# Three placements of sums, copies and weight splits around the seven-product projections of a one-core decoder layer

## The chip, the core and the metric

The kernel runs on one core of a Trainium2 chip. Its engines are called PE (matrix products), DVE and ACT (element-wise work), POOL, and SP (which issues the loads); each works through its own list of instructions in order. The metric is device time in microseconds (us) of one execution. Lower is better.

## What is computed

One layer: a norm, a combined input projection, three branches (attention, convolution, short convolution), a sum of the branches under sigmoid gates, an output projection with a residual, a second norm and a gated feed-forward part with a residual. The part that matters here:

```python
merged = g[:, :, 0] * y_a + g[:, :, 1] * y_b + g[:, :, 2] * y_c
x = x + merged @ w_o[l]
hf = rms_norm(x, ffn_norm_g[l]) @ w_ffn_in[l]
gt, up = jnp.split(hf, 2, axis=-1)
x = x + (jax.nn.silu(gt) * up) @ w_ffn_out[l]
```

There are 512 positions and 1024 channels; `w_o` is 1024 x 1024, `w_ffn_out` 2816 x 1024, all in f32.

## The kernel before

**Products.** A f32 operand is kept as two rounded tiles, a high part and a low part. ACT makes the high one with a cast (L81), DVE the low one with a subtraction (L82), and `mm3` (L92 on) makes one f32 product of three matmuls: high x high, low x high, high x low. In the records the weight's parts are `wh` and `wl`, and a matmul of 128x512 of any of these products is a row of L90.

**Seven products.** `merged @ w_o` and both halves of the last projection are cut into 2 x 2 blocks and done as a Strassen-like scheme of seven products instead of eight. The contraction goes in pairs of 128 rows: four pairs for `w_o`, six and then five for `w_ffn_out`. In what follows (j, p) is product p of pair j: two banks of three matmuls, six rows of L90. Block sums of the left side are made by `quarters` (L554 on), of the weights by DVE from the pieces b11, b12, b21, b22 of a pair. Products 1, 6 and 7 come first. At the change (`middle`, L606 on) ACT and DVE read their banks: the bank of product 7 gets -7 - (1 + 6), two new banks p5 are filled with the sum 1 + 6, and copies of product 7's old content (s7) are kept and added to the residual by `rest`. Products 2, 4, 5 and 3 then accumulate on top of what the banks hold, so product 4 of any pair needs the change of p7 done.

**Order.** PE's order is the one in which the code calls (`manual_schedule`). DVE, ACT, POOL and SP are ordered by a scheduler by priority; `tc.issue_after(i)` keeps an instruction behind i, `tc.high_priority` puts it forward. Each tile belongs to a ring of a few buffers (`wh` and `wl` three each, `raw` three), so a split also waits until PE has read the split that held its buffer.

**Around the change.** The last branch is `branch(1, ..., last=True)`: sixteen units, a gate and a product for each of eight column blocks. Behind its thirteenth unit stands `first_sums(0)`, which loads b11, b12 and b22 of pair 0 of `w_o` and forms t3 = b22 - b12 and t2 = t3 + b11 (L791, L792). For pairs 1 to 3 `first_sums` is called after the branch. PE's order there is (0,1), then (1,1), (0,6), (0,7), then (2,1), (1,6), (1,7), then (3,1), (2,6), (2,7), (3,6), (3,7), the change, and (0,2), (0,4), (1,2), (1,4) and so on (L853 on); t2 - b21 (L856) is the weight of product 4. Products 5 and 3 follow with the weight sums of L871, between them four transposes (`turn`, L819; its records are L822) for the second norm, and four more transposes after the first twelve matmuls of the feed-forward part. The residual adds are L862, L864, L884, L885 and L887; L624 is the add of `rest`. In `ffn_out` the sums for products 5 and 4 are L954 to L956, and the last two pairs of its second call are taken product by product, (3,5), (4,5), (3,3), (4,3), (3,4), (4,4), (3,2), (4,2); the final adds and stores are L986 and L988.

Of the kernel before, what the change touches and what calls it, by code (L numbers as in the profile page):

```python
# [35 lines left out]
def hybrid_layer(ctx, tc, x, mix_norm_g, w_in, q_norm_g, k_norm_g, w_attn_out, conf_dw_w,  # L36
# [537 lines left out]

    def seventh(a, w, banks, start):
        for i in range(2):
            mm3(banks[i], [t[:, i * P:(i + 1) * P] for t in a], w, start, True)
# [28 lines left out]
    def middle(p1, p6, p7):  # L606
# [4 lines left out]
        with tc.high_priority(offset=PRIO):  # L611
            for i in range(2):
                s1 = tmp()
                nc.scalar.copy(s1, p1[i])
                nc.vector.tensor_add(s2[i], p6[i], s1)
                nc.scalar.copy(p5[i], s2[i])
            for i in range(2):
                s7.append(tmp())
                nc.scalar.copy(s7[i], p7[i])
                change = nc.vector.scalar_tensor_tensor(p7[i], p7[i], -1.0, s2[i], ALU.mult,  # L620
                                                        ALU.subtract)
        def rest():
            for i in range(2):
                nc.vector.tensor_add(x1_at(i + 2, 1), s7[i], x1_at(i + 2, 1))  # L624
# [6 lines left out]
    def branch(g, w, a, last=False):  # L631
        for f4 in range(0, KT, 4):
            wy = once(lambda f4=f4: raw(w[:, f4 * P:(f4 + 4) * P], CT, 4 * P))
            for f2 in range(f4, f4 + 4, 2):
                wg = in_raw(4096 + g * D + f2 * P)
                for j in range(2):
# [7 lines left out]
                    def product(y, f=f, s=s):  # L644
                        if f not in merged:
# [126 lines left out]
    def after(*ins):  # L772
        stack = ExitStack()
        stack.enter_context(tc.high_priority())
        for i in ins:
            stack.enter_context(tc.issue_after(i))
        return stack

    def first_sums(j):
# [9 lines left out]
        with after(*last_sum):  # L789
            t3, t2 = tmp(), alloc("c")  # L790
# [16 lines left out]
    queue += units[:13] + [call(lambda: first_sums(0))] + units[13:]  # L807
# [32 lines left out]
    for j in range(n):  # L840
        if j:
            first_sums(j)
# [10 lines left out]
    b21 = [wo_piece(j, 1, 0) for j in range(n)]  # L853
    for j in range(n):
        with after(*[change][:j]):
            nc.vector.tensor_sub(t2s[j], t2s[j], b21[j])  # L856
# [10 lines left out]
    for j in range(n):  # L867
        b11, b12, b22 = wo_raw[j]
        with after(*[half][:j]):
            t1 = alloc("c")  # L870
            nc.vector.tensor_sub(t1, b12, b11)  # L871
        held.append(parts2(b22, t1))
        if j == 1:
            rest()
# [8 lines left out]
    for i in range(2):  # L883
        nc.vector.tensor_add(x1_at(i + 2, 1), x1_at(i + 2, 1), p5[i])  # L884
        nc.vector.tensor_add(x1_at(i, 1), x1_at(i, 1), p5[i])  # L885
    for i in range(2):
        nc.vector.tensor_add(x1_at(i, 1), x1_at(i, 1), p3[i])  # L887
# [41 lines left out]
    def ffn_out(j0, h, last):  # L929
# [23 lines left out]
        def t14(t1, t4):  # L953
            nc.vector.tensor_sub(t1, b12, b11)  # L954
            nc.vector.tensor_sub(t4, b22, b21)  # L955
            nc.vector.tensor_sub(t4, t4, t1)  # L956
# [3 lines left out]
        ends = n - 2 if last else n  # L960
        pieces, ws = [], []
        for j in range(n + 1):
            if j < n:
# [4 lines left out]
                pieces.append(w)  # L968
                two, three = parts(w[:, 1], "u" if last and j == n - 1 else None)
                ws.append({2: two, 3: three})  # L970
            if j:
                (b11, b12), (b21, b22) = [[pieces[j - 1][:, k, i] for i in range(2)]
                                          for k in range(2)]
                t1, t4 = parts(sums(t14, *[change][:j - 1]), "u" if last and j == n else None)
                ws[j - 1].update({5: t1, 4: t4})
            if j == 2:
                rest()
            now = [(j, p) for p in (2, 3) if j < ends] + [(j - 1, p) for p in (5, 4)
                                                          if 0 < j <= ends]
            if last and j == n:  # L980
                now = [(i, p) for p in (5, 3, 4, 2) for i in (n - 2, n - 1)]
            for i, p in now:
# [71 lines left out]
```

## Time and profile before

| | |
|---|---|
| median of three runs | 840.54 us (840.12 to 843.98) |
| the profiled execution | 839.71 us, its span 838.0 us |
| granted PE clock, mean | 0.997 |
| DVE / ACT busy | 76% / 49% of the span |
| stage of `w_o`, PE records | from 435.64 us to 482.95 us of the span |
| second call of `ffn_out`, from product 5 of pair 2 on | from 817.6 us to the end |

The records of PE overlap: a matmul of 128x512 is recorded with 0.39 us and the next one starts 0.23 us after it, so a busy share near 98% hides short waits, which are read from start times in the timeline and from the list of waits.

### The profile page before, as it was taken

The page shows a single profiled execution, that of the slowest core. Times are in us where ns is not written, and L with a number is a line of the kernel's source. Part 1 is how long each engine was busy: PE and PEld are TensorE (multiplying, and loading weights), DVE is VectorE, ACT ScalarE, POOL GpSimd, SP SyncE. Part 2 cuts the span into 40 slices and gives each one's busy share as a digit, 9 for nine tenths or more (in the row PEclk, how much of TensorE's full clock was granted, in tenths as well). Part 3 has the DMA queues.
Part 4 walks back from the last instruction along what each step waited for, and adds up shares of the span by engine and source line. Part 5 has one row for each costly group of instructions (what it writes and reads, how often), then busy time and mean ns, then how long its engine had stood idle before and what let it go on. Part 6 is the DMA issues. An engine that isn't in the chain of part 4 may idle for free.

```text
span 838.0 us, 9783 instructions
## 1 busy us (share of the span) xinstructions
PE 818.6 (98%) x3703; PEld 677.9 (81%) x3703; DVE 635.0 (76%) x952; ACT 410.9 (49%) x621; POOL 36.2 (4%) x60
## 2 busy tenths in 40 slices
PE   6999999999999999999998999999999999999997
PEld 6887887888888888888886778888888888888885
DVE  6598799897899999776578857555679865556796
ACT  6345698877664232573345554333345423333461
POOL 3100010002100000000000040000000000000000
PEclk9999999999999999999999999999999999999999
DMA  7333114112113143143241433332235733322452
GB/s 252 104 101 99 53 50 151 51 51 101 51 51 101 51 151 101 51 142 110 88 163 50 151 101 100 101 101 88 75 113 201 251 101 101 101 88 76 139 187 101
DMA packets 71468, 90.13 MB, mean 108 GB/s; under 512 B 2112, under 2 KB 56572, under 8 KB 71420
## 3 DMA queue, kind: packets, MB, share of 16 engines
q1 hardware_dynamic: 70252, 87.40, 31.3%
q10 hardware_dynamic: 1168, 2.10, 0.6%
q8 instruction: 29, 0.48, 0.2%
q14 instruction: 19, 0.16, 0.1%
HBM read 87.39 MB, written 2.10 MB: 107 GB/s over the span
## 4 chain that ended last, share of the span: by engine, by line
PE 89%; DVE 7%; issue 2%; ACT 1%; DMA 1%; SPq 0%; DVEq 0%; ACTq 0%
PE mm L90 75%; PE z L90 10%; PE o L90 3%; DVE wl L82 2%; DMA u<-in_w_o_dram 1%; ACT wh L81 1%; PE mm L297 1%; DVE cf L503 0%; DMA m<-in_x_dram 0%; PE z L297 0%; PE mm L822 0%; DVE tt L955 0%; DVE tt L956 0%; DVE tt L954 0%; DVE t L791 0%
## 5 line engine op out<-in xcount | busy, mean ns | idle before, releaser
L90 PE MATMUL mm<-u,wh 128*128 128x512 f32 x1536 | 474.9, 390 | 0.0
L90 PEld LDWEIGHTS mm<-u,wh 128*128 128x128 f32 x1536 | 287.2, 188 | 59.5 <-DVE u L304 0.6
L90 PE MATMUL mm<-u,wl 128*128 128x512 f32 x768 | 299.2, 390 | 0.0
L81 ACT CAST wh<-raw 128x1024 fp32r<-128x1024 f32 (+1 forms) x150 | 140.5, 937 | 240.5 <-PE mm L90 194.4
L82 DVE TENSOR_TENSOR wl<-raw,wh 128x1024 fp32r<-128x1024 f32 (+1 forms) x148 | 161.0, 1088 | 37.6 <-ACT wh L81 36.9
L90 PEld LDWEIGHTS mm<-u,wl 128*128 128x128 f32 x768 | 144.1, 188 | 30.1
L503 DVE SCALAR_TENSOR_TENSOR cf<-cf,cols_w,cf 128x512 f32<-128x512 f32 x120 | 89.8, 749 | 3.7 <-ACT cf L501 1.2
L916 DVE TENSOR_TENSOR t<-mm,cf 128x512 f32<-128x512 f32 x22 | 15.2, 691 | 59.7 <-PE mm L90 59.7
L90 PE MATMUL mm<-m,wh 128*128 128x512 f32 x128 | 39.4, 389 | 0.0
L81 ACT CAST wh<-tt 128x1024 fp32r<-128x1024 f32 x21 | 22.1, 1053 | 31.0 <-PE mm L90 16.5
L914 DVE TENSOR_TENSOR t<-mm,cf 128x512 f32<-128x512 f32 x22 | 15.1, 687 | 25.5 <-PE mm L90 25.4
L90 PE MATMUL mm<-wh,m 128*128 128x512 f32 x88 | 29.6, 392 | 0.0
L90 PEld LDWEIGHTS mm<-m,wh 128*128 128x128 f32 x128 | 24.0, 188 | 4.9
L82 DVE TENSOR_TENSOR wl<-tt,wh 128x1024 fp32r<-128x1024 f32 x21 | 25.6, 1220 | 2.9 <-ACT wh L81 2.8
L78 ACT ACTIVATE s<-s 128x384 f32<-128x384 f32 (+1 forms) x48 | 26.9, 561 | 1.1
L90 PE MATMUL z<-wh,m 128*128 128x512 f32 x72 | 26.0, 393 | 0.8 <-DVE z L620 0.8
L90 PE MATMUL mm<-m,wl 128*128 128x512 f32 x64 | 24.9, 389 | 0.0
L449 DVE SCALAR_TENSOR_TENSOR s<-z,s 128x384 f32<-128x384 f32 (+1 forms) x24 | 14.3, 598 | 11.6 <-ACT s L78 10.4
L834 POOL TENSOR_TENSOR cf<-cf,t 128x512 f32<-128x512 f32 x7 | 11.0, 1576 | 257.3 <-ACT t L832 257.1
L81 ACT CAST m<-t 128x512 fp32r<-128x512 f32 x21 | 13.1, 623 | 17.7 <-DVE t L560 11.3
L78 ACT ACTIVATE t<-t 128x512 f32<-128x512 f32 x31 | 19.6, 631 | 3.7 <-DVE t L914 3.6
L90 PEld LDWEIGHTS mm<-wh,m 128*128 128x128 f32 x88 | 16.8, 191 | 3.6
(301 smaller groups left out, 1135.6 us busy)
## 6 DMA issues: line engine op xcount, KB each, us to landing
raw<-in_w_in_dram SPq DMA_DIRECT2D x23, 1024.0 KB
raw<-in_w_ffn_in_dram SPq DMA_DIRECT2D x22, 1024.0 KB
raw<-in_w_ffn_out_dram SPq DMA_DIRECT2D x11, 1024.0 KB
raw<-in_w_ffn_out_dram SPq DMA_DIRECT2D x11, 512.0 KB
raw<-in_w_in_dram SPq DMA_DIRECT2D x10, 512.0 KB
raw<-in_w_ffn_out_dram SPq DMA_DIRECT2D x11, 256.0 KB
raw<-in_w_o_dram SPq DMA_DIRECT2D x9, 256.0 KB
m<-in_x_dram SPq DMA_DIRECT2D x8, 256.0 KB
```

Source lines behind the costliest of these rows:

```text
L78: table(nc.scalar.activation(o, i, f, **kw))
L81: (copy or nc.scalar.copy)(hi, src)
L82: return (sub or nc.vector.tensor_sub)(lo, src, hi.bitcast(F32))
L90: nc.tensor.matmul(o, lhsT, rhs, start=start, stop=stop, skip_group_check=True)
L297: nc.tensor.matmul(pts[f][:, t * P:(t + 1) * P], xblock(xt, t, f), diag, start=True, stop=True, skip_group_check=True)
L449: marks.append(nc.vector.scalar_tensor_tensor(t, z, 0.0, t, ALU.max, ALU.add))
L503: nc.vector.scalar_tensor_tensor(y, pad[:, n:n + S], w(n), y, ALU.mult, ALU.add)
L834: nc.gpsimd.tensor_add(sumsq, sumsq, s)
L914: nc.vector.tensor_mul(g, pg[0], rstd[0])
L916: nc.vector.tensor_mul(u, pu, rstd[0])
```

## The change

It reorders work and changes no product. It has five parts.

1. `first_sums(0)`, `(1)`, `(2)` are called between the last three units of the last branch instead of one before them and the others behind; t3 lies in the ring `cf` instead of `t`; the multiply of the very last product of the branch is kept behind the newest of these sums.
2. In `middle` the two copies into p5 come after the change of p7, and `rest` is kept behind a given instruction.
3. In `w_o`, product 4 of pair j is called behind product 2 of pair j + 1, all four t2 - b21 are kept behind the change (before: all but the first), and the sums t1 = b12 - b11 of pairs 0 to 2 are formed ahead of the first residual adds.
4. The last residual adds of `w_o` get a high priority.
5. In `ffn_out` the sums for products 5 and 4 are chained in the pairs' order, and for the last two pairs of the second call the weights of products 5 and 4 are split ahead of those of 2 and 3. PE's order in `ffn_out` stays.

```diff
@@ middle
                 nc.vector.tensor_add(s2[i], p6[i], s1)
-                nc.scalar.copy(p5[i], s2[i])
+            behind = []
             for i in range(2):
                 s7.append(tmp())
-                nc.scalar.copy(s7[i], p7[i])
-                change = nc.vector.scalar_tensor_tensor(p7[i], p7[i], -1.0, s2[i], ALU.mult,
-                                                        ALU.subtract)
-        def rest():
+                copied = nc.scalar.copy(s7[i], p7[i])
+                with after(*behind):
+                    change = nc.vector.scalar_tensor_tensor(p7[i], p7[i], -1.0, s2[i], ALU.mult,
+                                                            ALU.subtract)
+                behind = [change.ins]
+            with after(copied.ins):
+                for i in range(2):
+                    nc.scalar.copy(p5[i], s2[i])
+        def rest(*behind):
...
@@ branch
                     def product(y, f=f, s=s):
-                        if f not in merged:
+                        if last and f == KT - 1:
+                            with after(*last_sum):
+                                nc.vector.tensor_mul(s[0], y, s[0])
+                            nc.vector.tensor_add(merged[f], merged[f], s[0])
+                        elif f not in merged:
...
@@ first_sums and the last branch
-            t3, t2 = tmp(), alloc("c")
+            t3, t2 = alloc("cf"), alloc("c")
...
-    queue += units[:13] + [call(lambda: first_sums(0))] + units[13:]
+    queue += units[:13]
+    for j in range(3):
+        queue += [call(lambda j=j: first_sums(j)), units[13 + j]]
...
-        if j:
+        if j == n - 1:
             first_sums(j)
...
@@ w_o behind the change
+    fours = []
     for j in range(n):
-        with after(*[change][:j]):
+        with after(change):
             nc.vector.tensor_sub(t2s[j], t2s[j], b21[j])
         two, four = parts2(b21[j], t2s[j])
+        fours.append(four)
         seventh(mT[j][2], two, p1, False)
-        seventh(mT[j][4], four, p7, False)
-    with tc.high_priority(offset=PRIO):
+        for i in range(j - 1, j if j < n - 1 else n):
+            if i >= 0:
+                seventh(mT[i][4], fours[i], p7, False)
+    t1s, behind = [], []
+    for j in range(n - 1):
+        b11, b12, _ = wo_raw[j]
+        with after(*behind):
+            t1s.append(alloc("c"))
+            behind = [nc.vector.tensor_sub(t1s[j], b12, b11).ins]
+    with after(*behind):
...
-    for i in range(2):
-        nc.vector.tensor_add(x1_at(i + 2, 1), x1_at(i + 2, 1), p5[i])
+    with tc.high_priority(offset=PRIO):
+        for i in range(2):
+            nc.vector.tensor_add(x1_at(i + 2, 1), x1_at(i + 2, 1), p5[i])
...
@@ ffn_out
+            behind = formed + [change][:j]
+            ws[j][5], ws[j][4] = parts(sums(t14, *behind),
+                                       "u" if last and j == n - 1 else None)
...
+        for j in range(ends):
+            w23(j)
             if j:
+                w54(j - 1)
             if j == 2:
-                rest()
+                rest(change)
+            go((j, 2), (j, 3))
+            if j:
+                go((j - 1, 5), (j - 1, 4))
+        w54(ends - 1)
+        go((ends - 1, 5), (ends - 1, 4))
+        if last:
+            for fn in (w54, w23):
+                for j in (n - 2, n - 1):
+                    fn(j)
+            for p in (5, 3, 4, 2):
+                go((n - 2, p), (n - 1, p))
```

**First place: DVE at the end of the last branch.** Before, `raw_696` and `raw_703` hold the pieces of pairs 1 and 2, the `u` tiles those of pair 3 and the b21 pieces, and `t_675` is the last product's multiply:

```order
L856 TENSOR_TENSOR c_665_3678<-c_665_3678,u_727_3936 128x512
L651 TENSOR_TENSOR t_675_3738<-mm_678_3744,t_675_3738 128x512
L652 TENSOR_TENSOR v_473_2625<-v_473_2625,t_675_3738 128x512
L559 TENSOR_TENSOR t_679_3759<-v_473_2625 128x256
L82 TENSOR_TENSOR s_651_3625<-v_473_2625,s_651_3625 128x256
L560 TENSOR_TENSOR t_679_3759<-t_679_3759,v_473_2625 128x256
L561 TENSOR_TENSOR t_680_3760<-v_473_2625 128x256
L791 TENSOR_TENSOR t_697_3800<-raw_696_3796 128x512
L562 TENSOR_TENSOR t_680_3760<-v_473_2625,t_679_3759 128x256
L792 TENSOR_TENSOR c_698_3801<-t_697_3800,raw_696_3796 128x512
L791 TENSOR_TENSOR t_704_3836<-raw_703_3832 128x512
L82 TENSOR_TENSOR wl_702_3809<-t_697_3800,wh_701_3808 128x512
```

After the change, on DVE at the same place, with `raw_672` and `raw_679` for pairs 1 and 2 and L664 for the last product's multiply:

```order
L82 TENSOR_TENSOR wl_703_3813<-raw_672_3709,wh_702_3812 128x512
L673 TENSOR_TENSOR v_473_2625<-v_473_2625,t_662_3671 128x512
L805 TENSOR_TENSOR cf_680_3752<-raw_679_3748 128x512
L806 TENSOR_TENSOR c_681_3753<-cf_680_3752,raw_679_3748 128x512
L805 TENSOR_TENSOR cf_713_3874<-u_712_3872,u_711_3870 128x512
L806 TENSOR_TENSOR c_714_3875<-cf_713_3874,u_710_3868 128x512
L82 TENSOR_TENSOR wl_705_3817<-c_674_3714,wh_704_3816 128x512
L82 TENSOR_TENSOR wl_705_3817<-cf_673_3713,wh_704_3816 128x512
L664 TENSOR_TENSOR t_678_3746<-mm_684_3760,t_678_3746 128x512
L82 TENSOR_TENSOR wl_707_3841<-raw_679_3748,wh_706_3840 128x512
L665 TENSOR_TENSOR v_473_2625<-v_473_2625,t_678_3746 128x512
L82 TENSOR_TENSOR s_651_3625<-v_473_2625,s_651_3625 128x256
```

The weight sums of pairs 1 to 3, which stood behind the last multiply, now all stand ahead of it (those of pair 1 a few rows above the piece), and the first t2 - b21, which waited ahead of it for `u_727`, has gone to the change.

**Second place: the change of `w_o`.** PE before, just behind (0,2), with `wh_731` for pair 0 and `wh_733` for pair 1:

```order
L90 MATMUL z_694_3788<-wh_731_3945,m_603_3380 128x512
L90 MATMUL z_694_3788<-wl_732_3946,m_603_3380 128x512
L90 MATMUL z_694_3788<-wh_731_3945,m_604_3381 128x512
L90 MATMUL z_695_3789<-wh_731_3945,m_603_3380 128x512
L90 MATMUL z_695_3789<-wl_732_3946,m_603_3380 128x512
L90 MATMUL z_695_3789<-wh_731_3945,m_604_3381 128x512
L90 MATMUL mm_690_3784<-wh_733_3964,m_627_3503 128x512
L90 MATMUL mm_690_3784<-wl_734_3965,m_627_3503 128x512
```

PE after the change, at the same place:

```order
L90 MATMUL mm_696_3800<-wh_733_3958,m_627_3503 128x512
L90 MATMUL mm_696_3800<-wl_734_3959,m_627_3503 128x512
L90 MATMUL mm_696_3800<-wh_733_3958,m_628_3504 128x512
L90 MATMUL mm_697_3801<-wh_733_3958,m_627_3503 128x512
L90 MATMUL mm_697_3801<-wl_734_3959,m_627_3503 128x512
L90 MATMUL mm_697_3801<-wh_733_3958,m_628_3504 128x512
L90 MATMUL z_700_3804<-wh_731_3945,m_603_3380 128x512
L90 MATMUL z_700_3804<-wl_732_3946,m_603_3380 128x512
```

Product 2 of pair 1 has moved ahead of product 4 of pair 0. On DVE before, from the first change of p7 on:

```order
L620 SCALAR_TENSOR_TENSOR z_694_3788<-z_694_3788,t_721_3920 128x512
L82 TENSOR_TENSOR wl_736_3984<-u_729_3940,wh_735_3983 128x512
L624 TENSOR_TENSOR v_688_3781<-t_725_3930,v_688_3781 128x512
L620 SCALAR_TENSOR_TENSOR z_695_3789<-z_695_3789,t_722_3921 128x512
L856 TENSOR_TENSOR c_698_3801<-c_698_3801,u_728_3938 128x512
L856 TENSOR_TENSOR c_705_3837<-c_705_3837,u_729_3940 128x512
L856 TENSOR_TENSOR c_714_3875<-c_714_3875,u_730_3942 128x512
L82 TENSOR_TENSOR wl_734_3965<-c_698_3801,wh_733_3964 128x512
```

On DVE after the change, at the same place:

```order
L628 SCALAR_TENSOR_TENSOR z_700_3804<-z_700_3804,t_721_3920 128x512
L82 TENSOR_TENSOR wl_736_3978<-u_729_3940,wh_735_3977 128x512
L628 SCALAR_TENSOR_TENSOR z_701_3805<-z_701_3805,t_722_3921 128x512
L873 TENSOR_TENSOR c_665_3678<-c_665_3678,u_727_3936 128x512
L873 TENSOR_TENSOR c_674_3714<-c_674_3714,u_728_3938 128x512
L873 TENSOR_TENSOR c_681_3753<-c_681_3753,u_729_3940 128x512
L82 TENSOR_TENSOR wl_732_3946<-c_665_3678,wh_731_3945 128x512
L82 TENSOR_TENSOR wl_734_3959<-c_674_3714,wh_733_3958 128x512
```

The add of `rest` (L624) has gone from between the two changes, and pair 0's sum and low split for product 4 (`c_665`, `wl_732`) now stand behind them.

**Third place: DVE in the second call of `ffn_out`, behind its change.** Before, `tt_1230` belongs to pair 1 and `tt_1236` to pair 2:

```order
L954 TENSOR_TENSOR tt_1230_6611<-raw_1221_6567 128x512
L954 TENSOR_TENSOR tt_1236_6651<-raw_1227_6605 128x512
L82 TENSOR_TENSOR wl_1229_6608<-raw_1227_6605,wh_1228_6607 128x1024
L955 TENSOR_TENSOR tt_1236_6651<-raw_1227_6605 128x512
L955 TENSOR_TENSOR tt_1230_6611<-raw_1221_6567 128x512
L956 TENSOR_TENSOR tt_1236_6651<-tt_1236_6651 128x512
L956 TENSOR_TENSOR tt_1230_6611<-tt_1230_6611 128x512
L624 TENSOR_TENSOR v_688_3781<-t_1215_6544,v_688_3781 128x512
L82 TENSOR_TENSOR wl_1232_6616<-tt_1230_6611,wh_1231_6615 128x1024
```

On DVE after the change, `tt_1233` belongs to pair 2:

```order
L1002 TENSOR_TENSOR tt_1230_6611<-raw_1221_6567 128x512
L1003 TENSOR_TENSOR tt_1230_6611<-raw_1221_6567 128x512
L82 TENSOR_TENSOR wl_1229_6608<-raw_1227_6605,wh_1228_6607 128x1024
L1004 TENSOR_TENSOR tt_1230_6611<-tt_1230_6611 128x512
L1002 TENSOR_TENSOR tt_1233_6645<-raw_1227_6605 128x512
L1003 TENSOR_TENSOR tt_1233_6645<-raw_1227_6605 128x512
L82 TENSOR_TENSOR wl_1232_6616<-tt_1230_6611,wh_1231_6615 128x1024
L1004 TENSOR_TENSOR tt_1233_6645<-tt_1233_6645 128x512
```

The sums of two pairs, interleaved before, now follow each other pair by pair, and the add of `rest` (L624) has left this piece.

More of the change, by code (lines that the diff above doesn't have):

```diff
@@ L573, in spaces, with after @@
         return {k: list(v) for k, v in of.items()}
+    def after(*ins):
+        stack = ExitStack()
+        stack.enter_context(tc.high_priority(offset=PRIO))
+        for i in ins:
+            stack.enter_context(tc.issue_after(i))
+        return stack
     def seventh(a, w, banks, start):
@@ L868, in hybrid_layer @@
         b11, b12, b22 = wo_raw[j]
[L869 to L872, printed above, removed]
+        if j == n - 1:
+            with after(half):
+                t1s.append(alloc("c"))
+                nc.vector.tensor_sub(t1s[j], b12, b11)
+        held.append(parts2(b22, t1s[j]))
         if j == 1:
-            rest()
+            rest(half)
         if j == n - 2:
@@ L882, in hybrid_layer @@
                     turn(len(u2))()
-    for i in range(2):
-        nc.vector.tensor_add(x1_at(i + 2, 1), x1_at(i + 2, 1), p5[i])
-        nc.vector.tensor_add(x1_at(i, 1), x1_at(i, 1), p5[i])
-    for i in range(2):
-        nc.vector.tensor_add(x1_at(i, 1), x1_at(i, 1), p3[i])
+    with tc.high_priority(offset=PRIO):
+        for i in range(2):
+            nc.vector.tensor_add(x1_at(i + 2, 1), x1_at(i + 2, 1), p5[i])
+            nc.vector.tensor_add(x1_at(i, 1), x1_at(i, 1), p5[i])
+        for i in range(2):
+            nc.vector.tensor_add(x1_at(i, 1), x1_at(i, 1), p3[i])
     rstd = []
@@ L951, in ffn_out, with piece @@
         p3, p4 = [psum("mm") for _ in range(2)], p7
[L953 to L963, printed above, removed]
+        pieces, ws, formed = {}, [{} for _ in range(n)], []
+        def piece(j):
+            if j not in pieces:
                 with tc.high_priority():
@@ L967, in ffn_out, with w23, w54, t14 @@
                         "(k p) (n f) -> p k n f", p=P, n=2))
-                pieces.append(w)
-                two, three = parts(w[:, 1], "u" if last and j == n - 1 else None)
-                ws.append({2: two, 3: three})
+                pieces[j] = w
+            return pieces[j]
+        def w23(j):
+            ws[j][2], ws[j][3] = parts(piece(j)[:, 1], "u" if last and j == n - 1 else None)
+        def w54(j):
+            (b11, b12), (b21, b22) = [[piece(j)[:, k, i] for i in range(2)] for k in range(2)]
+            def t14(t1, t4):
+                nc.vector.tensor_sub(t1, b12, b11)
+                nc.vector.tensor_sub(t4, b22, b21)
+                formed[:] = [nc.vector.tensor_sub(t4, t4, t1).ins]
+            behind = formed + [change][:j]
+            ws[j][5], ws[j][4] = parts(sums(t14, *behind),
+                                       "u" if last and j == n - 1 else None)
+        def go(*which):
+            for i, p in which:
+                seventh(h[i][p], ws[i][p], {2: p1, 3: p3, 4: p4, 5: p5}[p], p == 3 and i == 0)
+        ends = n - 2 if last else n
+        for j in range(ends):
+            w23(j)
             if j:
[L972 to L975, printed above, removed]
+                w54(j - 1)
             if j == 2:
[L977 to L982, printed above, removed]
-                seventh(h[i][p], ws[i][p], {2: p1, 3: p3, 4: p4, 5: p5}[p], p == 3 and i == 0)
+                rest(change)
[10 more added lines that the diff above has]
+                go((n - 2, p), (n - 1, p))
         def add(i, c, p, final, op=nc.vector.tensor_add):
```

11 lines of the change are left out of this document (4 added, 7 removed).

## Prediction

> **What bounds the kernel now.** I read the page's span and chain first, then the list of what PE waited for in the two stages that the change touches, then PE's start times around each wait, and last DVE and ACT ahead of those.
>
> ```profile
> span 838.0 us, 9783 instructions
> PE 89%; DVE 7%; issue 2%; ACT 1%; DMA 1%; SPq 0%; DVEq 0%; ACTq 0%
> 259.45 82.96 PE mm L90 x366
> ```
>
> PE is 89% of the chain that ended last, so time can only be won where PE stands still. The third row, a piece of the chain, gives PE's pace: 82.96 / 366 = 0.227 us from one matmul of 128x512 to the next, 1.36 us for a product (j, p) of six. Whatever exceeds that pace is waiting.
>
> ```profile
> PE mm L90 <- DVE wl L82: 1.8, 1, 1.8
> PE z L90 <- DVE wl L82: 1.2, 1, 1.2
> PE z L90 <- DVE z L620: 0.8, 1, 0.8
> PE mm L822 <- DVE v L887: 0.8, 1, 0.8
> PE mm L90 <- ACT wh L81: 0.7, 1, 0.7
> ...
> PE z L90 <- DVE wl L82: 1.1, 2, 0.8
> PE z L90 <- ACT wh L81: 0.8, 1, 0.8
> ```
>
> These are PE's waits (us in total, times, longest). The first five are those from 435.6 to 489.2 us, the projection by `w_o` and the transposes behind it; the last two those from 798 to 835 us, the second call of `ffn_out`. The same list for 600 to 690 us, which holds the first call, is empty. As records overlap, the list counts each wait some 0.2 us short; start times show its whole size.
>
> **Term 1, the wait for (2,1).** PE (start, duration, engine, line, operation, count, idle before):
>
> ```profile
> 439.72 1.52 PE L90 MATMUL z<-l,m 128*128 128x512 f32 x6
> 441.92 0.49 PE L90 MATMUL mm<-wh,s 128*128 128x512 f32 x1 [0.68 <-ACT wh L81]
> 444.20 0.79 PE L90 MATMUL mm<-wl,s 128*128 128x512 f32 x1 [1.79 <-DVE wl L82]
> 447.35 0.65 PE L90 MATMUL mm<-wh,m 128*128 128x512 f32 x2
> 456.45 0.39 PE L90 MATMUL mm<-wh,m 128*128 128x512 f32 x1
> 445.00:446.00 1.00, 1.00 (x3) 0.79 (x3) 1.00 (x3) 0.00 (x0) 0.00 (x0) 0.50 0.00 0
> ```
>
> (0,7) is done at 439.72 + 1.36 = 441.08; the next matmul starts at 441.92 (0.84 lost), the one after it at 444.20 instead of 442.15 (2.05 lost). From 444.20 to 447.35 stand seven steps, 3.15 us where 7 x 0.227 = 1.59 would do: 1.56 lost. The last row, of the table by windows (start and end, length, busy time of PE, PEld, DVE, ACT and POOL, PE clock, DMA), shows why: the granted clock is 0.50 there. Together 4.45 us. (0,2) starts at 456.45.
>
> Why the weights were late:
>
> ```profile
> 435.51 0.69 DVE L856 TENSOR_TENSOR c<-c,u 128x512 f32<-128x512 f32 x1 [5.24 <-DMA u<-in_w_o_dram]
> 437.56 0.43 DVE L559 TENSOR_TENSOR t<-v 128x256 f32<-128x256 f32 x1
> 443.46 0.68 DVE L82 TENSOR_TENSOR wl<-raw,wh 128x512 fp32r<-128x512 f32 x1
> 428.13 3.17 SPq L769 DMA_DIRECT2D u<-in_w_o_dram  x7
> 459.46 1.88 DVE L856 TENSOR_TENSOR c<-c,u 128x512 f32<-128x512 f32 x3
> ```
>
> DVE stood 5.24 us behind one instruction, L856 of pair 0, which waits for a `u` tile whose load SP could issue only from 428.13 on; the multiply of the last product, its block sums and all weight sums of pairs 1 to 3 queued behind it, and the low part that PE needed at 441.31 was made at 443.46. The three L856 give DVE's step: (1.88 - 0.69) / 2 = 0.60 us, 0.09 less than one lasts; a 128x256 of 0.43 thus steps by 0.34. In the new order that L856 is gone and the sums of pairs 1 and 2 fill the hole. What waits for loads now is L805 and L806 of pair 3, on the first three `u` tiles, and behind them stand the last multiply and the split of (2,1). If the third lands when the fourth did (435.5), two sums, two splits for pair 1, the multiply and the split for (2,1) are six steps, 435.5 + 6 x 0.60 = 439.1, 2.2 us ahead of 441.31. Seven more such steps and six of 0.34, up to the split of (3,1), end at 445.3; (3,1) then stands at 441.08 + 3 x 1.36 = 445.16 and wants that split one matmul later, 445.39. So the whole 4.45 us go, with nothing to spare at (3,1): each us by which the third `u` tile comes later than 435.5 costs about one. It may come earlier (it is issued before the fourth) or later (one `raw` piece which before went last now goes ahead of it). **Value 4.4 us, bounds 3.4 and 4.5.**
>
> **Term 2, the change of p7 and product 4.**
>
> ```profile
> 455.55 0.62 PE L90 MATMUL z<-wh,l 128*128 128x512 f32 x2
> 456.44 0.58 ACT L619 COPY t<-z 128x512 f32<-128x512 f32 x1
> 457.06 0.70 DVE L620 SCALAR_TENSOR_TENSOR z<-z,t 128x512 f32<-128x512 f32 x1 [0.58 <-ACT t L619]
> 458.38 0.40 PE L90 MATMUL z<-wh,m 128*128 128x512 f32 x1
> 459.61 0.50 PE L90 MATMUL z<-wh,m 128*128 128x512 f32 x1 [0.84 <-DVE z L620]
> ```
>
> Before, (0,4) stops after its first bank: 459.61 - 458.61 = 1.0 us, and about 0.2 go in slower steps around it. ACT read p7 only at 456.44, though its first bank was finished at 455.55 + 0.39 = 455.94, because a copy to p5 stood ahead. In the new order that copy is behind, and I step through it with everything 4.45 us earlier. Bank ready 451.5; ACT's copy 0.58, 452.1; first change 452.7; the split of pair 2 behind it waits for ACT's cast, which waits for PE's last (3,7), and ends at 453.4; second change 454.0; three L873 (L856 before) 455.8; low split of pair 0, 0.68, 456.5. PE, with (1,2) now ahead of it, wants (0,4) at 456.45 - 4.45 + 2 x 1.36 = 454.7. The high part, cast by ACT once the first L873 is done, is there at 454.0 + 0.68 + 0.62 = 455.3 (0.6 lost), the low part at 456.5 instead of 455.5 (1.0 lost). So **a wait of about 1.6 us takes the place of 1.2**: the turn of (0,4) by one product wins 1.36 us, but the sum of pair 0, done early before, is now behind the change, with two more in front of the split. **Value -0.4; bounds +0.8 (only the low part late, 0.4 us in all) and -2.2 (1.8 us more, as if the clock fell, below).**
>
> **Term 3, the wait in (1,5).**
>
> ```profile
> 471.44 0.40 PE L90 MATMUL z<-wh,m 128*128 128x512 f32 x1
> 473.00 0.50 PE L90 MATMUL z<-wl,m 128*128 128x512 f32 x1 [1.16 <-DVE wl L82]
> 472.26 0.68 DVE L82 TENSOR_TENSOR wl<-c,wh 128x512 fp32r<-128x512 f32 x1
> ```
>
> 473.00 - 471.67 = 1.33 us, with the slow step behind it 1.4. The four residual adds and the sums t1 stood ahead of that split. In the new order t1 of pairs 0 to 2 come before the adds, and two of the four adds stand behind the split: from 456.5 I count 14 steps to it, 456.5 + 14 x 0.60 = 464.9, while (1,5) comes seven products after (0,4), at 457.7 + 9.5 = 467.2. 2.3 us of cover, so **1.4 us go, bounds 0.4 and 1.5** (a wait of 1 us comes back if DVE slips by over 3).
>
> **Term 4, the transposes.**
>
> ```profile
> 484.44 1.45 DVE L82 TENSOR_TENSOR wl<-raw,wh 128x1024 fp32r<-128x1024 f32 x1
> 486.75 1.82 PE L822 MATMUL mm<-identr,v 128*128 128x128 f32 x12 [0.79 <-DVE v L887]
> ```
>
> The first twelve feed-forward matmuls were through at 485.80, the transposes began at 486.75: 0.95 us. L887 stood behind a split of 128x1024 that started at 484.44; the new order has both L887 (L915) ahead of it. They then follow the split before, which waits for PE's (2,3), and end about 2.1 us after the end of the last product; PE wants them 2.85 us after it. **0.95 us, bounds 0 and 0.95.**
>
> **Term 5, the second `ffn_out`.**
>
> ```profile
> 808.81 1.22 DVE L82 TENSOR_TENSOR wl<-raw,wh 128x1024 fp32r<-128x1024 f32 x1
> 809.95 1.28 DVE L955 TENSOR_TENSOR tt<-raw 128x512 f32<-128x512 f32 x2
> 817.40 0.61 PE L90 MATMUL z<-wh,m 128*128 128x512 f32 x2
> 818.38 0.50 PE L90 MATMUL z<-wl,m 128*128 128x512 f32 x1 [0.36 <-DVE wl L82]
> 821.94 0.50 PE L90 MATMUL z<-wh,b 128*128 128x512 f32 x1 [0.75 <-ACT wh L81]
> 823.20 0.50 PE L90 MATMUL z<-wl,b 128*128 128x512 f32 x1 [0.76 <-DVE wl L82]
> 820.00:824.00 4.00, 2.49 (x11) 1.48 (x9) 4.00 (x7) 2.09 (x3) 0.00 (x0) 1.00 0.01 2
> ```
>
> (2,5) waits from 817.85 to 818.38, (3,5) from 821.03 to 821.94 and from 822.17 to 823.20: 0.53 + 0.91 + 1.03 + some 0.15 of slow steps = 2.6 us. A split of 128x1024 takes a step of 1.14 (808.81 to 809.95). In the new order DVE has eight sums and three such splits from the second change, which ends at 807.05, to the split for (2,5): 8 x 0.60 + 3 x 1.14 = 8.2, 815.3, 2.5 us ahead of the need. Three more sums and a split, 818.2, serve (3,5), wanted at 820.3 + 0.2. What is late next is the low split of row 1 for (4,3): two adds of `rest` and two final adds, the first of which waits for product 5's last bank at 822.5, now stand ahead of it. It ends at about 825.0 and PE wants it at 824.6: 0.4, with its slow step 0.5 us of new wait. **2.6 - 0.5 = 2.1 us, bounds 1.0 (the list's 1.9 halved, if the last split slips by another us) and 2.6.**
>
> In the first `ffn_out` (second row: PE's (1,5), a piece of the chain):
>
> ```profile
> 651.74 1.22 DVE L82 TENSOR_TENSOR wl<-tt,wh 128x1024 fp32r<-128x1024 f32 x1 [0.59 <-ACT wh L81]
> 653.20 0.68 PE z L90 x3
> ```
>
> PE waited for nothing there. The split for (1,5) ended at 652.96, 0.47 us ahead of the matmul at 653.43; by the new order, as in the second call, it comes some 2 us earlier. I put this stage at 0; if that cover went, each us of slip would cost one. SP's loads keep their number; POOL has nothing new. Behind the last matmul the adds and stores are unchanged.
>
> **Sum.** 4.4 - 0.4 + 1.4 + 0.95 + 2.1 = 8.45 us. The profiled execution took 839.71 us, 1.71 around its span; 839.71 - 8.45 = 831.3. It lies 0.83 under the median of the three runs shown (840.54), so the median by the same sum is 832.1; I take 831.6 between them.
>
> [...] At 445 to 446 the clock is 0.50, after 2.9 us of standing still broken by one matmul; at 820 to 824 it stays 1.00 with 0.91 + 1.03 us lost around one matmul. The new wait at (0,4), 0.6 + 1.0 around one matmul, is nearer to the second. [...]
>
> **The rivals.**
> - *The clock falls at (0,4).* For: its wait is split like the one that was followed by 0.50. Against: the 1.00 at 820 to 824. Price: the 1.56 us of term 1, so 833.2.
> - *The third `u` tile lands late.* It has one load more ahead of it. At 437.5 instead of 435.5 it costs 2 us, and such a wait at (3,1) may bring the 1.56 back: 833.6 to 835.2. Against: seven loads were issued within 3.17 us and the fourth had landed at 435.5.
> - *The time comes back in the feed-forward part*, PE arriving 6.3 us earlier at weights that come no earlier: 837.9. Against: from 489 to 817 us PE waits for nothing, and the `raw` buffers that those loads need come free earlier too. This would be no change by the bound below.
> - *Slower.* The last multiply is now tied behind sums that wait for loads, and DVE passes nothing by. One mechanism, at L806 of pair 3: from 435.5 on each us of delay is a us of PE, so it eats the 8.45 us at a landing near 444 and gives 845 from 448.5 on. Against: that is 20 us after the issue, where the fourth tile took under 7.5.
> - *The change doesn't do what it says*: the two orders show the moves on DVE, ACT and PE, so only a wait not seen could undo them; I count it in the third.
>
> **How the numbers follow.** Forecast 831.6, chance 0.60. Clock at (0,4) 0.13, late `u` 0.14, returned in the feed-forward part or some like loss 0.09, slower 0.04. The better ends of the terms sum to 10.35, 829.4; the poorer ones to 2.6, 837.1. As all five are not likely to fail together, I end at 836. The range is 829.4 to 836.0; it leaves out the last two cases and some of the tails, under 2 in 10. About 0.5% (4.2 us) is what a measurement of this kernel can tell from no change: faster by more 0.87, within it 0.09, slower by more 0.04.
>
> **What would show it.** Right: no PE wait between (0,7) and (0,2) and a clock of 1.00 throughout; a wait of 1 to 2 us for `wl` at (0,4); none in (1,5) and at the transposes; (2,5) and (3,5) without a wait, under 1 us at (4,3). Wrong: DVE standing over 8 us at L805 of pair 3, a granted clock of 0.50 around (0,4), or PE waits between 490 and 790 us, where there were none.

## The result and the profile after

The changed kernel takes 833.22 us (median of four runs, 832.6 to 834.08), the kernel before, timed beside it on the same chip, 840.56 us (840.12 to 843.98): a ratio of 0.9905, 95% interval 0.9877 to 0.9932. The profiled execution took 832.6 us, span 830.9. The forecast was 831.6, range 829.4 to 836.0. One timing of the run a_pair0_early below, 1174 us at a mean clock of 0.754, is left out of its median.

From the page of the changed kernel, the span and the chain that ended last, by engine:

```profile
span 830.9 us, 9787 instructions
PE 91%; DVE 6%; issue 1%; ACT 1%; DMA 0%; SPq 0%; DVEq 0%; ACTq 0%
```

The list of PE's waits in the changed kernel (us in total, times, longest), first from 424 to 492 us of the span, then from 798 to 835:

```profile
PE z L90 <- DVE wl L82: 0.7, 1, 0.7
PE mm L90 <- DVE u L843: 0.6, 1, 0.6
PE z L90 <- ACT wh L81: 0.6, 1, 0.6
PE mm L90 <- ACT t L848: 0.4, 1, 0.4
...
PE mm L90 <- DVE u L82: 0.3, 1, 0.3
```

Of the eight waits of before none is left as it was. (2,1), (1,5), (2,5), (3,5) and the first transposes wait for nothing. The two z rows are the wait foreseen at (0,4), the last row the one foreseen at (4,3). The second and fourth rows are new and were not foreseen: both stand in the first twelve feed-forward matmuls, between the projection by `w_o` and the transposes.

Where the time went is read from PE's start times, counted from the first row of each kernel's own `w_o` stage, because that row itself moves by up to 1.6 us from kernel to kernel (435.48 to 437.10) through the stages ahead, which most edits leave alone. From it to the first transposes it was 486.75 - 435.64 = 51.11 us and is 482.11 - 436.03 = 46.08: 5.03 us won. The transposes themselves run 0.35 us shorter, since before they caught up with the second residual add (1.82 against 1.47 us for the twelve). The second `ffn_out` wins 2.1: from (2,5) to the end of PE's work 14.24 us instead of 16.34. Against these, the stage starts 0.39 us later. Together 7.1 us, the difference of the spans. PE's clock is 1.00 in the whole stage, and from 490 to 790 us it waits for nothing, as before.

The three places in the changed kernel. First PE and then DVE and ACT around the end of the projection (start, duration, engine, line, operation, count, idle before):

```profile
478.35 0.73 PE L90 MATMUL mm<-u,wh 128*128 128x512 f32 x2 [0.42 <-ACT t L848]
480.51 0.39 PE L90 MATMUL mm<-u,wh 128*128 128x512 f32 x1
481.54 0.50 PE L90 MATMUL mm<-u,wh 128*128 128x512 f32 x1 [0.65 <-DVE u L843]
482.11 1.47 PE L838 MATMUL mm<-identr,v 128*128 128x128 f32 x12
```

```profile
477.26 1.23 DVE L82 TENSOR_TENSOR wl<-raw,wh 128x1024 fp32r<-128x1024 f32 x1
478.40 1.28 DVE L915 TENSOR_TENSOR v<-v,mm 128x512 f32<-128x512 f32 x2
479.60 1.22 DVE L82 TENSOR_TENSOR wl<-raw,wh 128x1024 fp32r<-128x1024 f32 x1
480.75 0.74 DVE L843 SCALAR_TENSOR_TENSOR u<-mm,cols,u 128x512 fp32r<-128x512 f32 x1
```

```profile
477.14 0.68 ACT L842 ACTIVATE u<-mm,cols 128x512 fp32r<-128x512 f32 x1
477.71 0.59 ACT L848 ACTIVATE t<-mm 128x512 f32<-128x512 f32 x1
```

The four calls of `turn` are counted 0 to 3. The last product ended at 477.76 by PE's pace. The first feed-forward product should start there, but its bank is read by the square of turn 2 (L848), which now stands behind turn 3's activation: 0.59 us lost. The eleventh matmul should start at 480.74 but needs the low part of turn 3 (L843 at 480.75), which on DVE now stands behind both L915 and a split of 128x1024: 0.80 us lost. With slow steps 1.63 us are lost between the end of the projection and the transposes, where 1.08 were before.

### The profile page after: what moved, and what is told of

Its sections match the earlier page's. It is cut to its first block, busy times and chain, and to the rows that moved or that the text cites. A ratio compares the mean times of both kernels' runs of the same rounds, so it can differ in the third digit from the quotient of the medians.

```text
span 830.9 us, 9787 instructions
## 1 busy us (share of the span) xinstructions
PE 816.1 (98%) x3703; PEld 677.6 (82%) x3703; DVE 635.3 (76%) x952; ACT 411.5 (50%) x621; POOL 35.1 (4%) x60
## 4 chain that ended last, share of the span: by engine, by line
PE 91%; DVE 6%; issue 1%; ACT 1%; DMA 0%; SPq 0%; DVEq 0%; ACTq 0%
PE mm L90 77%; PE z L90 10%; PE o L90 3%; DVE wl L82 1%; PE mm L297 1%; ACT wh L81 0%; DVE cf L503 0%; PE z L297 0%; DMA m<-in_x_dram 0%; PE mm L838 0%; DVE tt L1004 0%; DVE u L82 0%; DVE tt L1003 0%; DVE tt L1002 0%; DVE v L1034 0%
## 5 line engine op out<-in xcount | busy, mean ns | idle before, releaser
L90 PE MATMUL mm<-b,wh 128*128 128x512 f32 x64 | 19.7, 389 | 0.0
```

Of the source, the lines that this page charges most:

```text
L90: nc.tensor.matmul(o, lhsT, rhs, start=start, stop=stop, skip_group_check=True)
```

## The experiments

Eleven variants and the changed kernel once more ran, in three groups, each group beside the kernel before on one chip. The last two columns are from each kernel's trace, in us from the first row of its `w_o` stage to the first feed-forward matmul and to the first transposes.

| kernel | median, us | ratio to before (95%) | to feed-forward | to transposes |
|---|---|---|---|---|
| before | 840.56 to 841.8 in the groups | | 47.31 | 51.11 |
| changed | 833.22 | 0.9905 (0.9877 to 0.9932) | 42.32 | 46.08 |
| b_t2_behind | 846.65 | 1.0059 (1.0036 to 1.0082) | 51.78 | 55.58 |
| b_part1 | 836.27 | 0.9946 (0.9924 to 0.9967) | 42.93 | 46.74 |
| b_part5 | 838.02 | 0.9960 (0.9947 to 0.9974) | 47.25 | 51.06 |
| a_no_part1 | 834.96 | 0.9921 (0.9903 to 0.9939) | 43.95 | 47.71 |
| a_four_unturned | 835.43 | 0.9928 (0.9908 to 0.9948) | 43.71 | 47.47 |
| a_no_prio | 833.15 | 0.9904 (0.9885 to 0.9924) | 41.80 | 45.61 |
| a_low_only | 831.87 | 0.9890 (0.9873 to 0.9907) | 42.32 | 45.19 |
| a_turn_first | 831.35 | 0.9882 (0.9865 to 0.9898) | 41.89 | 44.77 |
| a_pair0_early | 831.35 | 0.9883 (0.9863 to 0.9902) | 40.54 | 44.29 |
| a_rest_behind | 832.08 | 0.9893 (0.9873 to 0.9912) | 42.32 | 46.07 |
| a_all | 829.02 | 0.9855 (0.9835 to 0.9876) | 40.06 | 42.91 |
| a_again (changed) | 833.22 | 0.9905 (0.9882 to 0.9928) | 42.34 | 46.09 |

### What made (2,1) late: the blocked instruction or the place of the sums?

**Before, with t2 - b21 of pair 0 behind the change (b_t2_behind).**

```diff
     for j in range(n):
-        with after(*[change][:j]):
+        with after(change):
             nc.vector.tensor_sub(t2s[j], t2s[j], b21[j])
```

> The kernel before with one edit: all four differences t2 - b21 stand behind the change of p7, so DVE no longer stands 5.24 us behind the L856 of pair 0. Theory A (term 1 as predicted: that one blocked instruction made the weights of (2,1) late): about 4.4 us go at (2,1), the clock stays at 1.00 there, and the new late split at (0,4) costs 1 to 3 us, so some 837 to 839 us. Rival B (behind the L856 stands the last multiply, which reads what PE finishes only at 435.6; DVE would stand there until 435.9 anyway, so it is the place of the sums behind that multiply that counts): DVE is only 0.2 to 0.3 us earlier, (2,1) still waits some 2.5 us, the clock falls or just holds, and with 1 to 3 us lost at (0,4) the time is 840 to 843 us.

It is slower than before. DVE and then PE in its timeline:

```profile
430.50 0.68 DVE L652 TENSOR_TENSOR v<-v,t 128x512 f32<-128x512 f32 x1
436.82 0.69 DVE L651 TENSOR_TENSOR t<-mm,t 128x512 f32<-128x512 f32 x1 [5.63 <-PE mm L90]
437.55 0.69 DVE L652 TENSOR_TENSOR v<-v,t 128x512 f32<-128x512 f32 x1
...
444.18 0.68 DVE L82 TENSOR_TENSOR wl<-raw,wh 128x512 fp32r<-128x512 f32 x1
```

```profile
442.63 0.50 PE L90 MATMUL mm<-wh,s 128*128 128x512 f32 x1 [0.48 <-ACT wh L81]
444.91 0.50 PE L90 MATMUL mm<-wl,s 128*128 128x512 f32 x1 [1.78 <-DVE wl L82]
...
460.09 0.49 PE L90 MATMUL z<-wh,m 128*128 128x512 f32 x1 [2.87 <-ACT wh L81]
461.85 0.79 PE L90 MATMUL z<-wl,m 128*128 128x512 f32 x1 [1.26 <-DVE wl L82]
```

The blocked L856 is gone, and DVE stands still just as long (5.63 us instead of 5.24), one instruction further: at the last multiply, L651, which reads what PE finishes when the stage begins (436.55 here). The split for (2,1) ends 8.3 us after the stage's first row, 8.5 before, and (2,1) loses 0.64 + 2.05 = 2.7 us again. At (0,4) 3.0 + 1.5 us are lost, and the clock falls to 0.50 there for 6.83 us (last section): from 461.85 to 468.19 fifteen steps took 6.34 us where 15 x 0.227 = 3.4 would do, another 2.9 lost. In the second `ffn_out` its clock is 0.50 once more, from 829.70 to 833.12 (last section), which in the profiled execution of the kernel before it is not: nine steps from 829.65 to 833.29 took 3.64 us where 2.04 would do, and these 1.6 us are part of the slower time. Rival B is borne out at (2,1); the loss at (0,4) is larger than either theory gave.

**Before, with the first part alone (b_part1).**

```diff
-    queue += units[:13] + [call(lambda: first_sums(0))] + units[13:]
+    queue += units[:13]
+    for j in range(3):
+        queue += [call(lambda j=j: first_sums(j)), units[13 + j]]
...
-        if j:
+        if j == n - 1:
             first_sums(j)
```

(and t3 in the ring `cf`, and the last multiply behind the newest sum, as in the change)

> The kernel before with the first part alone: the sums of pairs 1 to 3 stand ahead of the last multiply on DVE, and the difference t2 - b21 of pair 0 stays ahead of that multiply too, behind them, and still waits for its load. Rival B of the earlier runs (the place of the sums made (2,1) late, not the blocked instruction): (2,1) waits for nothing, the clock is 1.00 there, (0,4) and (1,5) wait as before, and 4.4 to 4.5 us go: ratio to the kernel before 0.9945 to 0.995. Theory A (the blocked instruction made it late, which is still there): under 1 us goes, ratio above 0.9985.

DVE in its timeline; here L798 and L799 are the sums, L865 is t2 - b21 of pair 0, L650 the last multiply:

```profile
432.55 0.69 DVE L799 TENSOR_TENSOR c<-cf,raw 128x512 f32<-128x512 f32 x1
435.76 0.69 DVE L798 TENSOR_TENSOR cf<-u,u 128x512 f32<-128x512 f32 x1 [2.53 <-DMA u<-in_w_o_dram]
436.49 0.69 DVE L799 TENSOR_TENSOR c<-cf,u 128x512 f32<-128x512 f32 x1
437.10 0.68 DVE L865 TENSOR_TENSOR c<-c,u 128x512 f32<-128x512 f32 x1
...
438.91 0.68 DVE L650 TENSOR_TENSOR t<-mm,t 128x512 f32<-128x512 f32 x1
```

The difference of pair 0 is still there, ahead of the multiply, and costs its own 0.6 us and no wait. (2,1) waits for nothing, and the way to the feed-forward part is 4.38 us shorter. The place of the sums, with the end of the slow clock that went with the wait, is the whole of term 1.

**The changed kernel with the first part undone (a_no_part1):** the same edit the other way round, in the changed kernel.

> The changed kernel with the first part undone: the sums of pairs 1 and 2 stand behind the last multiply again. All other parts stay. Theory A (the blocked L856 was the cause): nothing or under 0.5 us is lost, 833.2 to 833.7. Rival B (the place of the sums is the cause): DVE starts the sums at about 438.6; by the order there are two steps of 0.60 fewer than before ahead of the split for (2,1), so PE waits 0.8 for the high part and 0.5 for the low part there, 1.3 us if the clock holds at 1.00 and about 2.9 if it falls: 834.5 to 836.1.

(2,1) waits again, less than before and at a clock of 1.00:

```profile
443.06 0.50 PE L90 MATMUL mm<-wh,s 128*128 128x512 f32 x1 [0.48 <-ACT wh L81]
444.14 0.50 PE L90 MATMUL mm<-wl,s 128*128 128x512 f32 x1 [0.57 <-DVE wl L82]
```

1.63 us are lost to the feed-forward part and 1.74 in the medians. The first part is worth 4.4 us in the kernel before and 1.6 in the changed one: the parts do not add up one by one. Of the 2.8 us between them 1.56 are the slow clock, which did not come here, and most of the rest is that two steps of 0.60 fewer stand ahead of the split for (2,1): it starts 6.14 us after the last multiply here, 7.34 before.

### Product 4 and the change of p7

**Product 4 not turned (a_four_unturned).**

```diff
         seventh(mT[j][2], two, p1, False)
-        for i in range(j - 1, j if j < n - 1 else n):
-            if i >= 0:
-                seventh(mT[i][4], fours[i], p7, False)
+        seventh(mT[j][4], four, p7, False)
```

> The changed kernel with product 4 right behind product 2 of the same pair, as before: (0,4) stands one product, 1.36 us, earlier while its weights come at the same time. Theory (the turn wins what one product lasts): the wait at (0,4) grows from 0.73 + 0.93 to about 2.1 + 0.93 us, 834.6 if the clock holds. About 3 us of waiting broken by one matmul is what the kernel before had at (2,1), where the clock was 0.50 afterwards: if the length of the waiting decides, it falls here too and 1.56 us more go, 836.1. Rival (something later, such as the adds of pair 0 to 2, sets the end of the stage): no difference, 833.2.

```profile
456.70 0.51 PE L90 MATMUL z<-wh,m 128*128 128x512 f32 x1 [1.93 <-ACT wh L81]
457.85 0.50 PE L90 MATMUL z<-wl,m 128*128 128x512 f32 x1 [0.65 <-DVE wl L82]
454.00:460.00 6.00, 3.42 (x14) 2.29 (x13) 5.99 (x11) 4.08 (x9) 0.00 (x0) 1.00 0.00 0
```

2.09 + 0.92 = 3.0 us lost where the changed kernel loses 0.73 + 0.93, 1.39 more to the feed-forward part: what one product lasts. The clock (third number from the right in the last row, of the table by windows) stays at 1.00 through 3.0 us of waiting, more than the 2.9 after which it fell in the kernel before.

**Pair 0's difference early again, behind the splits of pair 3 (a_pair0_early).** Here `low2` holds the low splits that `parts2` made last, those of pair 3.

```diff
     for j in range(n):
-        with after(change):
+        with after(*([change] if j else low2[1:])):
             nc.vector.tensor_sub(t2s[j], t2s[j], b21[j])
```

> The changed kernel with the difference t2 - b21 of pair 0 and its split ahead of the change of p7 again, but now behind the weight sums and splits of pair 3, where nothing that PE waits for stands behind it. Theory (the wait at (0,4) comes from that sum and split being behind the change with two others between, not from the change itself): the change of the first bank is done at about 453.2 and PE wants (0,4) at 455.1, so the whole 1.76 us go, 831.5. Rival (the extra cast on ACT, 0.52 us, delays the copies of p7 and so the change, or the split of (1,4) becomes late): 0.5 us or more of wait stays, 832 or above.

No wait is left at (0,4). The way to the transposes is 1.79 us shorter than in the changed kernel, 831.35 against 833.22 in the medians. The change of p7 itself was in time; the wait of term 2 was the price of having moved pair 0's sum and split behind it.

### The loss ahead of the transposes

**Without the high priority of the last adds (a_no_prio).**

```diff
-    with tc.high_priority(offset=PRIO):
-        for i in range(2):
-            nc.vector.tensor_add(x1_at(i + 2, 1), x1_at(i + 2, 1), p5[i])
...
+    for i in range(2):
+        nc.vector.tensor_add(x1_at(i + 2, 1), x1_at(i + 2, 1), p5[i])
...
```

> The changed kernel with the high priority of the last residual adds (L912 to L915) taken away. Theory for the loss at the transposes: that priority put both L915 ahead of the low part of turn 3 (L843) on DVE and, by the order that follows from it, turn 3's activation ahead of the square of turn 2 on ACT. Without it the two new waits of PE (0.59 us lost ahead of the first feed-forward product, 0.8 us in its last third) go, and the wait of the transposes for the last adds comes back at about 0.95 us: 0.4 to 0.7 us faster than 833.2, 832.5 to 832.8. Rival (PE is simply early, and weights, loads and buffers come no earlier): the waits stay at the same places for other releasers, 833.2.

```profile
477.39 0.74 PE L90 MATMUL mm<-u,wh 128*128 128x512 f32 x2
480.02 0.39 PE L90 MATMUL mm<-u,wl 128*128 128x512 f32 x1
481.20 1.82 PE L838 MATMUL mm<-identr,v 128*128 128x128 f32 x12 [0.79 <-DVE v L914]
```

Both new waits are gone and the old one is back, as in the kernel before. The transposes start 0.47 us sooner, but the twelve take 1.82 us instead of 1.47, because they again run into the second add; 0.1 us is left, and the median is that of the changed kernel. So the high priority removed a wait of about 1.3 us (0.95 and 0.35) and made one of about 1.4 (0.59 and 0.80). The theory named the mechanism; its gain was too high by the 0.35.

**The low part of turn 3 ahead of the last two adds (a_low_only),** and **the square of turn 2 ahead of turn 3's activation too (a_turn_first).** `lows` is L843 of the newest turn, `squares` the newest L848; the third split of the feed-forward part is kept behind the adds. The first kernel has all but the line of `turn`.

```diff
-                    turn(len(u2))()
-    with tc.high_priority(offset=PRIO):
+                    turn(len(u2), *(squares if len(u2) == 3 else ()))()
...
+    with after(*lows):
         for i in range(2):
             nc.vector.tensor_add(x1_at(i, 1), x1_at(i, 1), p3[i])
```

> The changed kernel with the low part of turn 3 (L843) put ahead of the two last adds on DVE, and the third split of the feed-forward part behind them; ACT's order stays. Theory: the wait for u (0.8 us lost) goes, that for the square (0.59 us) stays, and the transposes want the adds at about 480.5 to 481.1 where DVE has them at 480.3: 0.8 us faster, 832.4. Rival (the first wait alone sets the end, the second is hidden behind the adds that the transposes need): under 0.3 us.

> As the kernel with the low part of turn 3 first, and the square of turn 2 ahead of turn 3's activation on ACT too. Theory: both waits go and the transposes come 2.7 us after the end of the last product without a wait: 1.4 to 1.6 us faster than 833.2, 831.6 to 831.8. Rival: the adds, now behind two later instructions, end at about 481 and the transposes wait 0.5 us or more again: 832.3.

PE's only wait in a_low_only from the end of the projection to the transposes, and in a_turn_first the rows at the same places:

```profile
478.67 0.73 PE L90 MATMUL mm<-u,wh 128*128 128x512 f32 x2 [0.42 <-ACT t L852]
481.54 1.47 PE L838 MATMUL mm<-identr,v 128*128 128x128 f32 x12
```

```profile
477.37 0.74 PE L90 MATMUL mm<-u,wh 128*128 128x512 f32 x2
480.02 0.39 PE L90 MATMUL mm<-u,wl 128*128 128x512 f32 x1
480.25 1.47 PE L838 MATMUL mm<-identr,v 128*128 128x128 f32 x12
```

The first wait goes with the order on DVE (0.89 us to the transposes), the second with the order on ACT (another 0.42), and neither comes back at the transposes. 1.31 us together, a tenth under the expected 1.4. In a_turn_first a wait of 0.2 us for a low part (L846) appears behind the second four transposes.

### The second ffn_out, and all together

**Before, with the fifth part alone (b_part5).**

> The kernel before with the new second half of ffn_out alone, which both calls use. Theory (term 5): the waits at (2,5) and (3,5) of the second call go, 0.5 us appears at (4,3), the first call stays without a wait: 2.1 us less, 838.4. Rival (the 2.1 us appear in the changed kernel only because PE comes to this stage earlier or because of the new order around the change of p7): under 1 us less, 839.6 to 840.5.

From the first row of `w_o` to PE's last six matmuls it is 831.43 - 436.53 = 394.90 us instead of 832.61 - 435.64 = 396.97: 2.07 us, term 5 as forecast. (2,5) and (3,5) wait for nothing, and (4,3) waits 0.4. The ratio gives 2.2 to 4.5 us, and the medians differ by 3.8, which is more than the trace. The seven executions of b_part5 have a mean granted clock of 0.997 to 1.000, the ten of the kernel before beside them 0.996 to 0.998. So a slow stretch at (3,5), which many executions of the kernel before may have (last section), may go with the wait there; no trace shows this.

**The residual adds of `rest` behind the weight splits (a_rest_behind).** `cut` is the last low split.

```diff
-            if j == 2:
+            if j == 2 and not last:
                 rest(change)
...
         if last:
             for fn in (w54, w23):
...
+            rest(change, cut[0].ins)
```

> The changed kernel with the two residual adds of rest (L640) in the second ffn_out put behind all weight splits. Theory: they and the two final adds that follow them set the end of the low split of row 1 that PE waits for at (4,3) (0.5 us lost); moved behind, that split ends at about 818.4 where PE wants it at 819.7, so 0.5 us goes, 832.7, and the final adds still end ahead of PE's last products, with the 4.03 us behind PE unchanged. Rival (ACT's casts set that split, not DVE's adds): 0.1 us or less.

DVE and then PE in its timeline:

```profile
817.43 1.29 DVE L84 TENSOR_TENSOR u<-raw,u 128x512 fp32r<-128x512 f32 x2
818.64 1.29 DVE L643 TENSOR_TENSOR v<-t,v 128x512 f32<-128x512 f32 x2
```

```profile
819.67 1.52 PE L93 MATMUL mm<-u,a 128*128 128x512 f32 x6
825.11 1.52 PE L93 MATMUL mm<-u,b 128*128 128x512 f32 x6
```

The splits end at 818.7, the six matmuls of (4,3) run through, and from the feed-forward's first matmul to PE's last six it is 346.51 us instead of 347.15: 0.6 us.

**The three repairs together (a_all),** beside **the changed kernel once more (a_again).**

> The changed kernel with the three repairs together: low part of turn 3 and square of turn 2 first (1.31 us by the trace of that kernel), pair 0's difference early (1.79 us), residual adds of rest behind the splits (0.5 us). Theory: they lie at three places of PE's chain and add up to 3.6 us, 829.6. Rival (PE, earlier by 3.1 us at the feed-forward part, meets loads that come no earlier there, or a repair shifts ACT's order for another): 1 us or more of it comes back, 830.6 or above.

> The changed kernel itself, beside the other three on the same chip, as their yardstick: 833.2 and the same waits at (0,4), ahead of the feed-forward part and at (4,3).

The list of PE's waits in a_all, from 424 us of the span to 840:

```profile
PE mm L93 <- DVE u L848: 0.2, 1, 0.2
```

One wait of 0.2 us is left from the projection to the end, behind the second four transposes. 829.02 against 833.22: 4.2 us in the medians, and by the traces of a_again and a_all 389.53 - 385.70 = 3.8 us from the stage's first row to PE's last six matmuls, where 3.6 were expected. This version is faster than both kernels, and 1.45% faster than the one before.

## Why the forecast held, and where it did not

- **The sum.** Forecast 8.45 us against the profiled execution; found 7.1. The difference is term 4 (1.15 us too high) and a stage that started 0.39 us later, less 0.2 that terms 1 to 3 brought beyond the 5.4 forecast for them.
- **Term 1, 4.4 us: the size right, the reason given for it wrong.** Found 4.49: (0,2) starts 16.32 us after the stage's first row instead of 20.81. The step that failed is "DVE stood 5.24 us behind one instruction, L856 of pair 0". That instruction was the one seen waiting, but not the one that cost: behind it stood the multiply that could not run before 436 us anyway (b_t2_behind), and with the sums in front the same instruction does no harm (b_part1). The stepping through the new order in the forecast put the sums in their new place, so the number came out right.
- **Term 2, -0.4: right.** Found 1.76 us lost instead of 1.2. The turn is worth 1.39 (a_four_unturned, forecast 1.36), the sum moved behind the change costs 1.79 (a_pair0_early). The rival of a falling clock did not come about: 1.00 at (0,4). In part that was luck: the forecast held against this rival that the clock stays at 1.00 after the 0.91 + 1.03 us at (3,5), and in b_t2_behind nearly the same waits were followed by 0.50.
- **Term 3, 1.4: right.** (1,5) has no wait.
- **Term 4, +0.95: this is the step that failed.** Found -0.2: 1.08 us lost ahead of the transposes and 0.35 in them before, 1.63 and none after. The forecast said "the new order has both L887 (L915) ahead of it", and that was so; the transposes wait for nothing. But it asked only who was served by the move and not who was overtaken. The low part of turn 3 stood in the same row of DVE's list and was wanted 0.45 us sooner than the transposes, by the last two matmuls ahead of them; the moved adds also let ACT's order turn, which the forecast had not looked at. a_no_prio, a_low_only and a_turn_first show both parts.
- **Term 5, 2.1: right to the tenth,** with the 0.5 at (4,3), and worth the same alone by the trace of b_part5.
- **The rivals.** The third `u` tile, feared to come late, let DVE go on at 434.95, and the last multiply ran at 437.49:

```profile
431.86 0.69 DVE L805 TENSOR_TENSOR cf<-raw 128x512 f32<-128x512 f32 x1 [1.71 <-DMA raw<-in_w_o_dram]
434.95 0.69 DVE L805 TENSOR_TENSOR cf<-u,u 128x512 f32<-128x512 f32 x1 [1.67 <-DMA u<-in_w_o_dram]
437.49 0.69 DVE L664 TENSOR_TENSOR t<-mm,t 128x512 f32<-128x512 f32 x1
```

Nothing of the time came back in the feed-forward part, and no blocked L806 appeared.

## What to carry to other kernels

An instruction that is seen waiting at the head of a queue is the cause only if what stands behind it could have run: take it away in thought and look at the next one's inputs. When an instruction is put forward on an engine, list everything that it overtakes and when PE wants each of those, not only who gets it sooner. And a move that only wins because something else moved too is worth a different amount in each order: 4.4 us in one kernel here, 1.6 in the other.

## What the runs showed of the hardware

In these runs the clock did not follow the length of the waiting. Two short windows, at the beginning and the end of the slow stretch, in the kernel before, in b_part5 and in b_t2_behind, and of the last two longer ones (start and end, length, busy times, and the clock as the third number from the right):

```profile
443.90:444.00 0.10, 0.00 (x0) 0.00 (x0) 0.10 (x1) 0.00 (x0) 0.00 (x0) 0.86 0.00 0
447.30:447.40 0.10, 0.10 (x2) 0.04 (x1) 0.01 (x1) 0.10 (x2) 0.00 (x0) 0.57 0.00 0
```

```profile
445.70:445.80 0.10, 0.10 (x2) 0.10 (x1) 0.10 (x1) 0.00 (x0) 0.00 (x0) 0.80 0.00 0
449.10:449.20 0.10, 0.10 (x2) 0.10 (x1) 0.10 (x2) 0.00 (x0) 0.00 (x0) 0.63 0.00 0
```

```profile
461.00:461.10 0.10, 0.00 (x0) 0.00 (x0) 0.10 (x1) 0.00 (x0) 0.00 (x0) 0.82 0.00 0
467.80:467.90 0.10, 0.10 (x1) 0.10 (x1) 0.00 (x0) 0.00 (x0) 0.00 (x0) 0.54 0.00 0
444.00:447.41 3.41, 2.50 (x11) 2.08 (x12) 3.38 (x7) 1.04 (x2) 0.00 (x0) 1.00 0.00 0
829.70:833.12 3.42, 3.42 (x10) 2.68 (x9) 1.65 (x4) 0.00 (x0) 0.00 (x0) 0.50 0.00 0
```

Taken as a mean of 1.00 and 0.50, the clock of 0.86 over 0.10 us puts the last 0.028 us at 0.50; by this estimate the stretch of the kernel before begins at 443.97, and likewise ends at 447.39: 3.41 us. In b_part5 it is 445.76 to 449.17, again 3.41, and begins 0.9 us after PE had its weights; in b_t2_behind 461.06 to 467.89, 6.83, twice that. The waits at (2,1) are the same 0.64 + 2.05 us in b_part5 and in b_t2_behind, yet in the second the clock stays at 1.00 there (the row from 444.00 on). It stays so through the 2.09 + 0.92 of a_four_unturned too. At (3,5) it is the other way round: after 0.93 + 1.03 us of waiting b_t2_behind has 0.50 from 829.70 to 833.12 (the last row), and the kernel before stays at 1.00 after 0.91 + 1.03. So the stretches at 0.50 seen here lasted 3.41, 3.41, 3.42 and 6.83 us, and of the waits of 1.9 to 3.0 us broken by one matmul some were followed by one and some were not; what decides it was not shown.

Ahead of the falls PE did not stand still throughout: in the 3.41 us before 443.97 (before), 445.76 (b_part5) and 829.70 (b_t2_behind) it worked, by its pace of 0.227 us a matmul, for 0.75, 0.98 and 1.31 us.

How often one kernel falls can be estimated, since the mean granted clock of each timed execution is on record. One stretch of 3.41 us lowers it by 0.002 (half of 3.41 in 838 us); what is slow behind PE's last matmul lowers it by up to 0.001 (0.999 in the profiled execution of the changed kernel, whose clock is 1.00 through all of PE's work up to 826.8 us and 0.89 from there to the end at 830.9). By this estimate, 0.996 stands for two stretches, 0.997 and 0.998 for one, 0.999 and more for none. Of 24 executions of the kernel before in the three groups, 13 have 0.996 and took 841.67 to 842.98 us, ten have 0.997 or 0.998 and took 839.83 to 840.76, and one has 0.999 and took 839.45. The eight of the changed kernel have 0.999 or 1.000. So the 1.56 us that term 1 put down to the slow clock are missing in one of these 24, and more than half seem to have a second stretch, which the profiled one does not have. That its place is (3,5), as in b_t2_behind, is not shown: no such execution was profiled.
